# First stage of a hybrid decoder block: conditioning tiles loaded ahead of weight tiles, a quarter of three tiles' modulation products on TensorE, and a new hand-written order up to the second half's rows

## The chip, the cores and the metric

The program runs on one core of one Trainium2 chip. The metric is the device time of one execution in microseconds. Before the change three timed executions gave 1150.15, 1150.58 and 1151.71 us, median 1150.58 us.

The core has five instruction streams, each working through its own list in order: TensorE (PE, with its weight loads shown as PEld), VectorE (DVE), ScalarE (ACT), GpSimd (POOL) and SyncE (SP, which here only starts DMA transfers). A stream goes on to its next instruction only when what that instruction waits for has happened. So the order of each list matters as much as its length.

## The reference

The block has an input of 1024 rows (positions) by 1024 features, in float32, and a conditioning vector `c`. What the first stage has to compute is this part:

```python
c_act = jax.nn.silu(c)
mod = jnp.einsum('bd,de->be', c_act, w_ada[layer]) + b_ada[layer]
shift_m, scale_m, gate_m, shift_f, scale_f, gate_f = jnp.split(mod[:, None, :], N_MOD, axis=-1)
u = rms_norm(h, g_mix[layer]) * (1.0 + scale_m) + shift_m
proj = jnp.einsum('bsd,de->bse', u, w_in[layer])
u_pool, z = proj[..., OFF_POOL:OFF_Z], proj[..., OFF_Z:OFF_XBC]
u_xbc, u_dt = proj[..., OFF_XBC:OFF_DT], proj[..., OFF_DT:]
```

After it come a pooling mixer, a state-space mixer with a short causal convolution, an output projection and a squared-ReLU feed-forward part. They fill the rest of the execution, and the change doesn't touch them.

## The kernel before, in words

The rows are treated in two halves of 512 (row tiles 0 to 3 and 4 to 7, of 128 rows each). The 1024 features are eight tiles of 128, numbered `k`. Products in float32 are made as three products of split numbers: `hi` is the number rounded to TensorE's faster float32 form, `lo` is the rest, and `hi*hi + hi*lo + lo*hi` is summed.

**Opening, to about 17 us.** SP loads the first four row tiles (`tok`), then the first tile of input weights (`raw`, 128x768), then conditioning weights (`adaw`, one 128x8x256 tile for each `k`). For each row tile ACT squares and sums (`square_sum`), DVE divides (`rsqrt_cols`), POOL raises to the power -1/2 (`rst`), and DVE or ACT multiplies the row by it (`row_scale`). `cact` is silu(c), made on DVE from a transposed parameter tile. `busy(n)` are n products of ones whose result nobody reads.

**One feature tile `k`.** `ada_dve(k, ...)` on DVE forms the weighted sum over the eight slices of `adaw[k]`: two plain products, six multiply-and-adds into two accumulators (`adaa`), and for most `k` one addition of the two. `ada_pe(k)` on TensorE multiplies that by ones, which sums over partitions, and `ada_cols(k)` on DVE makes two columns of it, `sh_m` and `sc_m` (shift and scale). Then ACT, with these two columns, turns the transposed rows (`stage`) into `u` (its `hi` part) and `utmp`, and DVE subtracts for its `lo` part (`ada_lo`). The weight tile `raw` is cast to `hi` on ACT and subtracted to `lo` on DVE. `stage_x(k)` transposes the rows on TensorE and copies them on ACT.

**Chunks.** `chunk(k)`, for `k` 0 to 7, has 18 products of 128x512 on TensorE (`part`), into six PSUM banks `accs` that stay in use through the whole stage. Between them stand `stage_x(k + 2)`, the loads of tile `k + 2`, and the conditioning of tile `k + 1`: `ada_pe(k + 1)`, then `ada_hi`, `ada_lo`, `ada_dve(k + 2)`. So `ada_dve(k + 2)` stands on DVE behind the columns of `k + 1`, and the columns of `k + 2` need `ada_dve(k + 2)`.

**The second half's rows.** Tiles 4 to 7 are loaded in `chunk(5)`. `row_rs` and `row_scale` treat two of them after `chunk(6)` and two after `chunk(7)` (table `XS`). Then `z0_tok(t)` multiplies a row tile by the first z columns (24 products of 128x256), with weights `zu` in four units of `hi` and `lo`; `u_half1(k)` transposes and modulates the second half's rows; `conv_half` copies an `accs` bank to SBUF, which frees it; `feat` is a further 24 products of 128x512.

**What sets the order.** Inside `with pinned(...)` the listed engines keep the order of the program's lines. Outside, a scheduler may move instructions. Before, `chunk(0)` to `chunk(5)` are pinned on four engines, and chunks 6 and 7 are not pinned. The table `UH` says after which `z0_tok` which `u_half1` are placed. Buffers are limited: three for `adaw`, two for `raw`, three for `hi` and `lo`, eight PSUM banks.

Of the kernel before, what the change touches and what calls it, by code (L numbers as in the profile page):

```python
# [9 lines left out]
F32 = mybir.dt.float32  # L10
# [30 lines left out]
UH = ((), (), (0, 1), (2, 3, 4), (5, 6, 7))  # L41
NPF = 2
XS = {6: (4, 5), 7: (6, 7)}
# [22 lines left out]
def tile_hybrid_block(  # L66
# [282 lines left out]
    ada_a = {}  # L349

    def ada_dve(k, ks):
        if ks[0] == 0:
            ada_a[k] = [stp.tile([P, 256], F32, name="adaa", tag="adaa", bufs=4) for _ in range(2)]
        ada_reduce(ada_w[k], ada_a[k], 256, ks)
        if ks[-1] == KD - 1 and k > 1:
            a, b = ada_a[k]
            dve.tensor_tensor(out=a, in0=a, in1=b, op=ALU.add)
            ada_a[k] = [a]

    def ada_pe(k):  # L360
        ps = bank()
        pa, pb = ps[:, 0:HD], ps[:, HD:2 * HD]
        for f, p_ in enumerate((pa, pb)):
            fs = slice(f * P, (f + 1) * P)
            for i, a in enumerate(ada_a[k]):
                pe.matmul(p_, lhsT=a[:, fs], rhs=ones[:, 0:HD], start=i == 0, stop=i == len(ada_a[k]) - 1)
        ada_cols(k, pa, pb)
# [35 lines left out]
    kw = []  # L403
    with pinned((act, dve, pool, pe)):
# [9 lines left out]
        row_rs(0)  # L414
        row_scale(0, False)
        row_rs(1)
# [6 lines left out]
        row_rs(2)  # L423
# [6 lines left out]
        row_rs(3)  # L430
        row_scale(2, True, slice(HW, D))
        spec = specs.popleft()
        raw0 = stp.tile([P, 768], F32, name="raw", tag="raws", bufs=2)
        for c0, c1, src in spec[2]:
            sp.dma_start(out=raw0[:, c0:c1].unsqueeze(1), in_=src)
        ada_load(0)
        ada_load(1)
        acc = [stp.tile([P, 256], F32, name="adaa", tag="adaa", bufs=4)[:, :P] for _ in range(2)]
        hi0 = stp.tile([P, 768], F32R, name="hi", tag="hi", bufs=3)
        lo0 = stp.tile([P, 768], F32R, name="lo", tag="lo", bufs=3)  # L440

        def dve_f0(ks):
            for k in ks:
                a = acc[k % 2]
                src = ada_w[0][:, k, 0:P]
                if k < 2:
                    dve.tensor_scalar(out=a, in0=src, scalar1=cact[:, k:k + 1], scalar2=None, op0=ALU.mult)
                else:
                    dve.scalar_tensor_tensor(out=a, in0=src, scalar=cact[:, k:k + 1], in1=a,
                                             op0=ALU.mult, op1=ALU.add)  # L450
# [15 lines left out]

        lo_0(0, 384)
        pe_f1(range(2))
        busy(3)
        pe_f1(range(2, 4))  # L470
        busy(2)
        stage_x(0)
        pe_f1(range(4, 6))
        busy(1)
        pe_f1(range(6, KD))
        for i in range(2):
            pe.matmul(pa, lhsT=acc[i], rhs=ones[:, 0:HD], start=i == 0, stop=i == 1)
        ada_cols(0, pa, pb)
        tmp = ada_hi(0)
        lo_0(384, 768)  # L480
        ada_lo(0, tmp)
        stage_x(1)
        busy(WARM2)
        ada_dve(1, range(KD))
        kw.append([(hi0, lo0)])
        kw.append(get(1, 0))
        accs = [bank() for _ in range(6)]

    def part(k, f, i):
        whi, wlo = kw[k][0]  # L490
        u = uT[k][0]
        fs = slice(f * P, (f + 1) * P)
        w, v = ((whi, 0), (wlo, 0), (whi, 1))[i]
        pe.matmul(accs[f], lhsT=w[:, fs], rhs=u[:, v, :], start=k == 0 and i == 0, stop=k == KD - 1 and i == 2)  # L494
# [3 lines left out]
    def chunk(k):  # L498
        if k == 0:
# [5 lines left out]
        for f, i in todo[:6]:  # L505
            part(k, f, i)
        if k + 2 < KD:
            stage_x(k + 2)
            split = unit_load(*specs.popleft())
            ada_load(k + 2)  # L510
        for f, i in todo[6:cut]:
# [14 lines left out]
        if k == 5:  # L526
# [6 lines left out]
            zpre.extend(unit_load(*specs.popleft()) for _ in range(NPF))  # L533
# [4 lines left out]
        for t in XS.get(k, ()):  # L538
            row_rs(t, pool)
            row_scale(t, t == 7)  # L540
# [3 lines left out]
    chunk(6)  # L544
    chunk(7)
# [1106 lines left out]
```

## Time and profile before

| | us |
|---|---|
| median of three timed executions | 1150.58 |
| profiled execution, device time | 1151.4 |
| its span, first to last instruction | 1149.7 |
| PE busy | 1131.9 (98% of the span) |
| DVE busy | 828.6 (72%) |
| ACT busy | 564.2 (49%) |
| POOL busy | 147.6 (13%) |
| granted TensorE clock, mean | 0.998 |
| first product with weights (`part`) starts | 17.24 |
| columns of tile 7 (`sh_m`) start | 56.20 |
| first transposes for the second half start | 71.43 |

Times inside the execution are counted from the start of its span. A row of the timeline has the start, the duration, the engine, the line, the operation, `out<-in`, the shape, the count of merged instructions, and in brackets how long the engine was idle just before it and what ended that. Instructions on one engine overlap a little, so starts are compared with starts. A float32 product whose operands aren't split appears as two MATMUL instructions. An engine called SPq, ACTq or POOLq is that engine's queue of DMA starts.

### The profile page before, as it was taken

The numbers are of one execution on the slowest core, as the hardware profiler recorded it, in microseconds if no ns is written. First come the engines' busy times: TensorE is split into PE (matmuls) and PEld (weight loads), VectorE is DVE, ScalarE is ACT, GpSimd is POOL, SyncE is SP. The second block draws the span as 40 slices with busy tenths as digits, with TensorE's granted clock in tenths as the row PEclk, the third lists the DMA queues.
The fourth block names the chain that finished last, engine by engine and source line by source line (L and its number), as shares of the span: only waits on it lengthen the run. The fifth ranks groups of instructions, "written<-read, shape, count | busy, mean of one in ns | idle before, by whom it ended". The sixth has DMA issues, their size and how long they took to land.

```text
span 1149.7 us, 15130 instructions
## 1 busy us (share of the span) xinstructions
PE 1131.9 (98%) x5475; PEld 937.7 (82%) x5475; DVE 828.6 (72%) x1244; ACT 564.2 (49%) x988; POOL 147.6 (13%) x188
## 2 busy tenths in 40 slices
PE   8989999999999999999999999999999999999997
PEld 8788887877898878878788888888888888888886
DVE  6969889958778576666987666665458744586985
ACT  5577665534354424545774444444434344434373
POOL 3021235325300012022000000000100000000030
PEclk9999999999999999999999999999999999999999
DMA  9922432323166767763165434442599835775832
GB/s 281 306 62 74 131 101 80 94 87 106 67 190 195 230 189 230 242 198 114 36 238 195 172 139 164 144 158 88 211 387 342 306 93 161 251 250 188 269 125 92
DMA packets 124091, 200.72 MB, mean 175 GB/s; under 512 B 8656, under 2 KB 65776, under 8 KB 121968
## 3 DMA queue, kind: packets, MB, share of 16 engines
q1 hardware_dynamic: 122656, 196.24, 51.2%
q0 software_dynamic: 1120, 3.21, 0.8%
q8 instruction: 43, 0.70, 0.3%
q14 instruction: 32, 0.26, 0.1%
q10 hardware_dynamic: 240, 0.30, 0.1%
HBM read 159.81 MB, written 39.91 MB: 174 GB/s over the span
## 4 chain that ended last, share of the span: by engine, by line
PE 76%; DMA 9%; DVE 7%; ACT 3%; issue 2%; POOL 1%; SPq 0%; POOLq 0%; DVEq 0%; ACTq 0%
PE bank L240 67%; DMA raw<-in_w_ada_dram 4%; PE bank L760 2%; DMA raw<-in_w_out_dram 2%; PE bank L494 2%; DVE acc L868 2%; DMA adaw<-in_w_ada_dram 1%; DMA raw<-ypool_d 1%; DVE lo L192 1%; PE bank L764 1%; PE bank L134 1%; PE bank L757 1%; PE bank L835 1%; POOL rst L176 0%; ACT hi L191 0%
## 5 line engine op out<-in xcount | busy, mean ns | idle before, releaser
L240 PE MATMUL bank<-dlo,dhi 128*128 128x512 f32 (+1 forms) x464 | 177.2, 382 | 0.0
L240 PE MATMUL bank<-dhi 128*128 128x512 f32 (+1 forms) x464 | 177.2, 382 | 0.0
L240 PE MATMUL bank<-dhi,dlo 128*128 128x512 f32 (+1 forms) x464 | 177.1, 382 | 0.0
L240 PE MATMUL bank<-u,hi 128*128 128x512 f32 x464 | 149.6, 403 | 0.0
L1471 ACT CAST dhi<-fr 128x1024 fp32r<-128x1024 f32 x56 | 58.9, 1052 | 143.3 <-PE bank L240 110.0
L1472 DVE TENSOR_TENSOR dlo<-fr,dhi 128x1024 fp32r<-128x1024 f32 x56 | 68.5, 1223 | 80.4 <-ACT dhi L1471 80.2
L240 PE MATMUL bank<-hi,ym 128*128 128x512 f32 x384 | 124.4, 396 | 1.1 <-DVE tok L1089 1.1
L191 ACT CAST hi<-raw 128x512 fp32r<-128x512 f32 (+2 forms) x101 | 62.9, 633 | 87.2 <-DMA raw<-in_w_out_dram 39.7
L240 PEld LDWEIGHTS bank<-u,hi 128*128 128x128 f32 x464 | 85.9, 188 | 22.1 <-issue 4.8
L240 PEld LDWEIGHTS bank<-dhi 128*128 128x128 f32 x464 | 87.2, 188 | 17.1
L240 PEld LDWEIGHTS bank<-dlo,dhi 128*128 128x128 f32 x464 | 87.2, 188 | 16.9
L240 PEld LDWEIGHTS bank<-dhi,dlo 128*128 128x128 f32 x464 | 87.2, 188 | 16.7
L192 DVE TENSOR_TENSOR lo<-raw,hi 128x512 fp32r<-128x512 f32 (+2 forms) x101 | 74.8, 747 | 29.1 <-ACT hi L191 28.6
L240 PE MATMUL bank<-E,whl 128*128 128x512 f32 x384 | 92.6, 391 | 0.1
L240 PE MATMUL bank<-u,lo 128*128 128x512 f32 x232 | 90.7, 391 | 0.0
L240 PEld LDWEIGHTS bank<-hi,ym 128*128 128x128 f32 x384 | 72.1, 188 | 17.0 <-DVE tok L1089 1.5
L240 PEld LDWEIGHTS bank<-E,whl 128*128 128x128 f32 x384 | 71.7, 188 | 16.5 <-DVE whl L1245 0.9
L176 POOL TENSOR_TENSOR rst<-ssq,mhalf 128x1 f32<-128x1 f32 (+2 forms) x27 | 26.8, 995 | 395.8 <-DVE ssq L175 363.7
L240 PE MATMUL bank<-u,whl 128*128 128x512 f32 x312 | 75.6, 390 | 0.0
L240 PE MATMUL bank<-lo,ym 128*128 128x512 f32 x192 | 74.9, 390 | 0.3 <-DVE lo L192 0.3
L240 PEld LDWEIGHTS bank<-u,whl 128*128 128x128 f32 x312 | 58.5, 188 | 12.5 <-DVE whl L1245 0.4
L1245 DVE TENSOR_TENSOR whl<-wraw,whl 128x512 fp32r<-128x512 f32 x58 | 40.0, 689 | 36.9 <-ACT whl L1240 36.8
(272 smaller groups left out, 2200.7 us busy)
## 6 DMA issues: line engine op xcount, KB each, us to landing
f_d<-tok SPq DMA_DIRECT2D x16, 1792.0 KB, 7.0
wr<-in_w_down_dram SPq DMA_DIRECT2D x56, 512.0 KB, 5.1
fr<-f_d SPq DMA_DIRECT2D x53, 512.0 KB, 4.3
raw<-in_w_ada_dram SPq DMA_DIRECT2D x64, 256.0 KB, 3.1
wraw<-in_w_up_dram SPq DMA_DIRECT2D x15, 1024.0 KB, 5.3
raw<-in_w_in_dram SPq DMA_DIRECT2D x48, 256.0 KB, 3.3
raw<-in_w_out_dram SPq DMA_DIRECT2D x48, 256.0 KB, 3.3
tok<-in_x_dram SPq DMA_DIRECT2D x16, 512.0 KB, 5.9
```

The lines of the kernel that those rows point to most:

```text
L134: return pe.transpose(dst, src, ident)
L176: pool.tensor_tensor(out=rst[:, a:b], in0=m, in1=mhalf[:, :b - a], op=ALU.pow)
L191: act.copy(hi[:, :n], raw[:, :n])
L192: dve.tensor_tensor(out=lo[:, :n], in0=raw[:, :n], in1=hi[:, :n].bitcast(F32), op=ALU.subtract)
L240: pe.matmul(ps, lhsT=st_, rhs=mv, start=first and i == 0, stop=last and i == 2, skip_group_check=more)
L494: pe.matmul(accs[f], lhsT=w[:, fs], rhs=u[:, v, :], start=k == 0 and i == 0, stop=k == KD - 1 and i == 2)
L757: pe.matmul(po, lhsT=C[:, cs], rhs=states[g], start=True, stop=True)
L760: pe.matmul(py[:, hh * HD:(hh + 1) * HD], lhsT=Ms[hh // 4][:, (hh % 4) * P:(hh % 4 + 1) * P], rhs=xdt[:, hh * HD:(hh + 1) * HD], start=Tru ...
L868: dve.scalar_tensor_tensor(out=acc[0], in0=raw, scalar=cact[:, k:k + 1], in1=acc[0], op0=ALU.mult, op1=ALU.add)
L1245: dve.tensor_tensor(out=t_[:, 1], in0=src, in1=t_[:, 0].bitcast(F32), op=ALU.subtract)
L1471: act.copy(hi, src)
L1472: dve.tensor_tensor(out=lo, in0=src, in1=hi.bitcast(F32), op=ALU.subtract)
```

## The change

It does six things, all ahead of the second half's rows.

1. SP's list has the conditioning tile ahead of the weight tile throughout (`ada_load(0)`, `w_load()`, `ada_load(1)`, `w_load()`, ...).
2. For tiles 0, 1 and 2 the slices 6 and 7 of the weighted sum leave DVE. TensorE multiplies those two slices directly by a column of `cact` (`ada_pass`). Tile 2's two accumulators are summed on TensorE without DVE's addition (`ada_sum`), as those of tiles 0 and 1 already were.
3. `u`'s `hi` part is made by DVE for tiles 0 and 1.
4. The weight's cast stands ahead of the columns on ACT, and the weight's subtraction (`w_lo`) right behind the columns on DVE. Chunk 1 has the same order of products as chunk 0.
5. POOL starts four small parameter transfers a second time, between the powers of the first four rows.
6. Chunks 6 and 7 and the second half's rows are pinned on ACT, DVE and POOL. All four row tiles stand behind `chunk(7)`, all four units of z weights are loaded and split ahead of them, and `UH` starts one `z0_tok` earlier.

```diff
-UH = ((), (), (0, 1), (2, 3, 4), (5, 6, 7))
-NPF = 2
-XS = {6: (4, 5), 7: (6, 7)}
+UH = ((), (0,), (1, 2), (3, 4), (5, 6, 7))
...
+    direct = {0: (6, 7), 1: (6, 7), 2: (6, 7)}
...
+    def ada_pass(p_, k, i, f, start, stop):
+        pe.matmul(p_, lhsT=ada_w[k][:, i, f * P:(f + 1) * P], rhs=cact[:, i:i + 1].broadcast_to([P, HD]),
+                  start=start, stop=stop)
+
+    def ada_sum(p_, k, f, start, stop):
+        for i, a in enumerate(ada_a[k]):
+            pe.matmul(p_, lhsT=a[:, f * P:(f + 1) * P], rhs=ones[:, 0:HD], start=start and i == 0,
+                      stop=stop and i == len(ada_a[k]) - 1)
...
-        affine_act(u[:, 0, :], src, k)
-        (affine_dve if k == 0 else affine_act)(tmp, src, k)
-        return tmp
+        (affine_dve if k < 2 else affine_act)(u[:, 0, :], src, k)
+        return tmp, src
...
-        row_rs(0)
+        row_ssq(0)
+        row_pow(0)
+        pool.dma_start(out=pr1[80:84, :], in_=rows(pool_scale))
+        row_ssq(1)
         row_scale(0, False)
-        row_rs(1)
+        row_pow(1)
+        pool.dma_start(out=dtb, in_=dt_bias.broadcast_to([P, HEADS]))
...
+        row_ssq(2)
+        row_pow(2)
+        pool.dma_start(out=nea, in_=a_log.broadcast_to([P, HEADS]))
...
+        ada_dve(0, range(6))
         pe_f1(range(2))
...
+        ada_sum(pa, 0, 0, True, False)
         pe_f1(range(6, KD))
...
+        for k in (6, 7):
+            ada_pass(pa, 0, k, 0, False, k == 7)
         ada_cols(0, pa, pb)
...
         if k + 1 < KD:
+            w_hi(k + 1)
             ada_pe(k + 1)
-            tmp = ada_hi(k + 1)
-            if k + 2 < KD:
-                ada_dve(k + 2, range(4))
-            ada_lo(k + 1, tmp)
-            if k + 2 < KD:
-                ada_dve(k + 2, range(4, KD))
-                kw.append(split())
+            tmp, src = ada_hi(k + 1)
+            affine_act(tmp, src, k + 1)
+            w_lo(k + 1)
+            if k == 0:
+                ada_lo(k + 1, tmp)
+                ada_dve(k + 2, range(KD))
+            else:
+                if k + 2 < KD:
+                    ada_dve(k + 2, range(3))
+                ada_lo(k + 1, tmp)
+                if k + 2 < KD:
+                    ada_dve(k + 2, range(3, KD))
...
-            zpre.extend(unit_load(*specs.popleft()) for _ in range(NPF))
+            zpre.extend(unit_load(*specs.popleft()) for _ in range(4))
...
-        for t in XS.get(k, ()):
-            row_rs(t, pool)
-            row_scale(t, t == 7)
     with pinned((act, dve, pool, pe)):
         for k in range(6):
             chunk(k)
-    chunk(6)
-    chunk(7)
+    with pinned((act, dve, pool)):
+        chunk(6)
+        chunk(7)
+        for t in range(4, 8):
+            row_ssq(t)
+            row_pow(t, pool)
+            row_scale(t, t == 7)
```

The diff says little about where things come to stand, so here are three places of the built programs. Line numbers of the changed kernel differ from those of the kernel before.

First, DVE's list for one feature tile in the middle of the stage, from one pair of columns to the next, before (`adaa` are the accumulators of the following tile's weighted sum, `lo<-raw,hi` is the weight's subtraction, `u<-utmp,u` the rows' subtraction):

```order
L371 TENSOR_TENSOR sh_m<-bank,pc 128x1
L372 SCALAR_TENSOR_TENSOR sc_m<-bank,pc 128x1
L260 TENSOR_SCALAR adaa<-adaw,cact 128x256 x2
L262 SCALAR_TENSOR_TENSOR adaa<-adaw,cact,adaa 128x256 x2
L392 TENSOR_TENSOR u<-utmp,u 128x512
L262 SCALAR_TENSOR_TENSOR adaa<-adaw,cact,adaa 128x256 x4
L357 TENSOR_TENSOR adaa<-adaa 128x256
L192 TENSOR_TENSOR lo<-raw,hi 128x768
L371 TENSOR_TENSOR sh_m<-bank,pc 128x1
```

and the same stretch of the changed kernel:

```order
L384 TENSOR_TENSOR sh_m<-bank,pc 128x1
L385 SCALAR_TENSOR_TENSOR sc_m<-bank,pc 128x1
L475 TENSOR_TENSOR lo<-raw,hi 128x768
L258 TENSOR_SCALAR adaa<-adaw,cact 128x256 x2
L260 SCALAR_TENSOR_TENSOR adaa<-adaw,cact,adaa 128x256
L404 TENSOR_TENSOR u<-utmp,u 128x512
L260 SCALAR_TENSOR_TENSOR adaa<-adaw,cact,adaa 128x256 x5
L360 TENSOR_TENSOR adaa<-adaa 128x256
L384 TENSOR_TENSOR sh_m<-bank,pc 128x1
```

The weight's subtraction went from behind the last addition to ahead of the weighted sum, and nothing stands any more between that addition and the next columns.

Second, POOL's list in the opening. Before, from the last of the small transfers on (`rst` are the powers, one for each of the first four rows):

```order
L410 DMA adaa<-in_pool_scale_dram 4x128
L411 DMA dtb<-in_dt_bias_dram 128x16
L412 DMA nea<-in_a_log_dram 128x16
L413 DMA dsk<-in_d_skip_dram 128x16
L176 TENSOR_TENSOR rst<-ssq,mhalf 128x1 x4
```

and changed:

```order
L421 DMA adaa<-in_pool_scale_dram 4x128
L422 DMA dtb<-in_dt_bias_dram 128x16
L423 DMA nea<-in_a_log_dram 128x16
L424 DMA dsk<-in_d_skip_dram 128x16
L174 TENSOR_TENSOR rst<-ssq,mhalf 128x1
L427 DMA adaa<-in_pool_scale_dram 4x128
L174 TENSOR_TENSOR rst<-ssq,mhalf 128x1
L431 DMA dtb<-in_dt_bias_dram 128x16
L174 TENSOR_TENSOR rst<-ssq,mhalf 128x1
L440 DMA nea<-in_a_log_dram 128x16
L174 TENSOR_TENSOR rst<-ssq,mhalf 128x1
L449 DMA dsk<-in_d_skip_dram 128x16
```

The first list of transfers stayed whole. Each repeated one writes the same tile as its first copy, so it carries a wait for that copy to have landed, and the next row's power stands behind it.

Third, ACT's list from the modulation of feature tile 7 (`u`, `utmp`) to the first work on the second half's transposed rows. Before:

```order
L191 CAST hi<-raw 128x512 x2
L381 ACTIVATE u<-stage,sh_m,sc_m 128x512
L381 ACTIVATE utmp<-stage,sh_m,sc_m 128x512
L244 ACTIVATE utmp,ssq<-tok 128x1024 x4
L191 CAST hi<-raw 128x512
L323 ACTIVATE tok<-tok,rst 128x1024
L191 CAST hi<-raw 128x512 x3
L570 COPY craw<-bank 128x512 x2
```

and changed:

```order
L394 ACTIVATE utmp<-stage,sh_m,sc_m 128x512
L189 CAST hi<-raw 128x512 x4
L242 ACTIVATE utmp,ssq<-tok 128x1024 x4
L189 CAST hi<-raw 128x512
L323 ACTIVATE tok<-tok,rst 128x1024
L189 CAST hi<-raw 128x512
L645 ACTIVATE zt<-bank 128x240
L601 COPY craw<-bank 128x512 x2
```

Four casts of z weights now stand between `utmp` and the four squares (two of them stood ahead of `u`, and two behind the squares), and the two copies that free PSUM banks come behind one `zt` of the first z rows. On TensorE, the products of `z0_tok` that stood between the last parts of chunk 6 and of chunk 7 now stand behind chunk 7, and so does the rest of them.

More of the change, by code (lines that the diff above doesn't have):

```diff
@@ L349, in tile_hybrid_block @@
     ada_a = {}
+    direct = {0: (6, 7), 1: (6, 7), 2: (6, 7)}
     def ada_dve(k, ks):
+        own = [i for i in ks if i not in direct.get(k, ())]
         if ks[0] == 0:
-            ada_a[k] = [stp.tile([P, 256], F32, name="adaa", tag="adaa", bufs=4) for _ in range(2)]
-        ada_reduce(ada_w[k], ada_a[k], 256, ks)
-        if ks[-1] == KD - 1 and k > 1:
+            n = P if k == 0 else 256
+            ada_a[k] = [stp.tile([P, 256], F32, name="adaa", tag="adaa", bufs=4)[:, :n] for _ in range(2)]
+        ada_reduce(ada_w[k], ada_a[k], P if k == 0 else 256, own)
+        if ks[-1] == KD - 1 and k not in direct:
             a, b = ada_a[k]
@@ L362, in ada_pe @@
         pa, pb = ps[:, 0:HD], ps[:, HD:2 * HD]
+        own = direct.get(k, ())
         for f, p_ in enumerate((pa, pb)):
-            fs = slice(f * P, (f + 1) * P)
-            for i, a in enumerate(ada_a[k]):
-                pe.matmul(p_, lhsT=a[:, fs], rhs=ones[:, 0:HD], start=i == 0, stop=i == len(ada_a[k]) - 1)
+            for i in own:
+                ada_pass(p_, k, i, f, i == own[0], False)
+            ada_sum(p_, k, f, not own, True)
         ada_cols(k, pa, pb)
@@ L429, in tile_hybrid_block, with w_load, w_hi, w_lo @@
         row_scale(2, False, slice(0, HW))
-        row_rs(3)
+        row_ssq(3)
+        row_pow(3)
+        pool.dma_start(out=dsk, in_=d_skip.broadcast_to([P, HEADS]))
         row_scale(2, True, slice(HW, D))
[L432 to L435, printed above, removed]
         ada_load(0)
-        ada_load(1)
[L438 to L450, printed above, removed]
+        raws = {}
+        def w_load():
+            k = len(raws)
+            raw = stp.tile([P, 768], F32, name="raw", tag="raws", bufs=2)
+            for c0, c1, src in specs.popleft()[2]:
+                sp.dma_start(out=raw[:, c0:c1].unsqueeze(1), in_=src)
+            raws[k] = raw
+        w_load()
+        ada_load(1)
+        w_load()
+        whl = {}
+        def w_hi(k, parts=((0, 768),)):
+            if k not in whl:
+                whl[k] = [stp.tile([P, 768], F32R, name=n, tag=n, bufs=3) for n in ("hi", "lo")]
+            for c0, c1 in parts:
+                act.copy(whl[k][0][:, c0:c1], raws[k][:, c0:c1])
+        def w_lo(k, parts=((0, 768),)):
+            hi, lo = whl[k]
+            for c0, c1 in parts:
+                dve.tensor_tensor(out=lo[:, c0:c1], in0=raws[k][:, c0:c1], in1=hi[:, c0:c1].bitcast(F32),
+                                  op=ALU.subtract)
         pa, pb = bank()[:, 0:HD], bank()[:, 0:HD]
@@ L506, in chunk @@
             part(k, f, i)
+        if k == 0:
+            stage_x(1)
         if k + 2 < KD:
             stage_x(k + 2)
[L509 removed]
             ada_load(k + 2)
+            w_load()
         for f, i in todo[6:cut]:
```

41 lines of the change are left out of this document (17 added, 24 removed).

## The prediction

> **What bounds the kernel now.** I read the busy shares first:
>
> ```profile
> PE 1131.9 (98%) x5475; PEld 937.7 (82%) x5475; DVE 828.6 (72%) x1244; ACT 564.2 (49%) x988; POOL 147.6 (13%) x188
> ```
>
> TensorE is busy for 98% of the span; 17.8 us are left. So time can be won where TensorE waits, and lost wherever another engine makes it wait more. The shares don't say how close the others are in the changed stage. For that I read the timeline of one chunk, with DVE's steps and TensorE's modulation products among them:
>
> ```profile
> 33.61 0.16 DVE L371 TENSOR_TENSOR sh_m<-bank,pc 128x1 f32<-128x1 f32 x1
> ...
> 33.68 0.21 DVE L372 SCALAR_TENSOR_TENSOR sc_m<-bank,pc 128x1 f32<-128x1 f32 x1
> ...
> 33.81 0.61 DVE L260 TENSOR_SCALAR adaa<-adaw,cact 128x256 f32<-128x256 f32 x2
> ...
> 34.33 0.88 DVE L262 SCALAR_TENSOR_TENSOR adaa<-adaw,cact,adaa 128x256 f32<-128x256 f32 x2
> ...
> 35.54 0.69 DVE L392 TENSOR_TENSOR u<-utmp,u 128x512 fp32r<-128x512 f32 x1 [0.33 <-ACT utmp L381]
> ...
> 36.15 1.67 DVE L262 SCALAR_TENSOR_TENSOR adaa<-adaw,cact,adaa 128x256 f32<-128x256 f32 x4
> ...
> 37.85 0.42 DVE L357 TENSOR_TENSOR adaa<-adaa 128x256 f32<-128x256 f32 x1
> ...
> 38.20 0.95 DVE L192 TENSOR_TENSOR lo<-raw,hi 128x768 fp32r<-128x768 f32 x1
> ...
> 38.42 0.63 PE L366 MATMUL bank<-ones,adaa 128*128 128x64 f32 x4
> ...
> 39.09 0.16 DVE L371 TENSOR_TENSOR sh_m<-bank,pc 128x1 f32<-128x1 f32 x1
> ```
>
> The columns come 5.48 us apart (33.61 to 39.09), and this is a closed loop: columns, weighted sum with the rows' subtraction in it, addition (ends 38.27), products of ones (38.42 to 39.05), next columns. The weight's subtraction lies in the shade: DVE runs it while it would wait for those products. TensorE's side of one chunk, from the chain of waits:
>
> ```profile
> 39.05 2.96 PE bank L494 x12
> 42.01 0.44 PE bank L134 x4
> 42.45 1.40 PE bank L494 x6
> ...
> 43.91 0.63 PE bank L366 x4
> ```
>
> That is 5.43 us. TensorE and DVE's loop are 0.05 us apart here: what lengthens either lengthens the chunk. The waits that TensorE has in the first 130 us, from the view of waits (us in total, times, longest):
>
> ```profile
> PE bank L134 <- ACT cv L250: 1.1, 1, 1.1
> ...
> PE bank L240 <- DVE lo L192: 0.9, 1, 0.9
> ...
> PE bank L240 <- ACT hi L191: 0.9, 1, 0.9
> ...
> PE bank L494 <- ACT u L381: 0.8, 2, 0.4
> ...
> PE bank L366 <- DVE adaa L357: 0.5, 1, 0.5
> ```
>
> 4.2 us in all: the most that these edits could take from TensorE's visible waits behind the opening.
>
> **The change part by part.**
>
> *Opening.* The first copy of the transfer that POOL repeats first, its time from issue to landing, and what hangs on POOL's powers:
>
> ```profile
> 5.25 0.50 POOL L410 DMA_DIRECT2D adaa<-in_pool_scale_dram  x1
> ...
> 8.94 0.55 POOL L176 TENSOR_TENSOR rst<-ssq,mhalf 128x1 f32<-128x1 f32 x1 [0.93 <-DVE ssq L175]
> ...
> 9.53 0.75 DVE L325 TENSOR_SCALAR tok<-tok,rst 128x1024 f32<-128x1024 f32 x1 [0.33 <-POOL rst L176]
> ...
> 12.22 0.48 DVE L325 TENSOR_SCALAR tok<-tok,rst 128x512 f32<-128x512 f32 x1 [0.27 <-POOL rst L176]
> ...
> 12.63 1.84 DVE L449 SCALAR_TENSOR_TENSOR adaa<-adaw,cact,adaa 128x128 f32<-128x128 f32 x6
> ...
> 16.00 0.16 DVE L371 TENSOR_TENSOR sh_m<-bank,pc 128x1 f32<-128x1 f32 x1 [1.06 <-PE bank L477]
> ...
> 16.39 0.55 DVE L377 TENSOR_SCALAR utmp<-stage,sc_m,sh_m 128x512 f32<-128x512 f32 x1
> ...
> 17.24 1.67 PE L494 MATMUL bank<-u,hi 128*128 128x512 f32 x6 [0.39 <-ACT u L381]
> ```
>
> ```profile
> adaa<-in_pool_scale_dram POOLq DMA_DIRECT2D x1, 2.0 KB, 4.7
> ```
>
> The first copy lands at 5.25 + 4.7 = 9.95. The repeated one waits for that, then takes 0.50 to issue, so row 1's power starts at 10.45 and not at 8.94, and row 1's scaling on DVE at 11.1 and not at 9.53: +1.57. Behind the power stand the other powers; behind the scaling stand `cact`, the scaling of rows 2 and 3 and the weighted sum. Their old spacing (row 3's scaling 2.69 behind row 1's) leaves room for the other two issues if their copies, sent 0.5 and 1.1 us after the first, have landed too, which I take. Row 3 is scaled at 13.8. Now the whole weighted sum of tile 0 stands behind it, 0.41 later: two plain products (0.4) and four multiply-adds (two thirds of 1.84, 1.2) end at 15.85. Then TensorE has two products of ones and four direct ones to do. Their price is in the next fence: four products start 0.81 before the next thing, 0.2 each, so 1.2, and 0.3 for the wait and the tail. Columns at 17.35 instead of 16.00. `u` is now made by DVE (0.39 behind, 0.55 long) instead of ACT, so the first weight product is at 18.35: **+1.1**. The conditioning tile comes ahead of the weight tile, but it isn't what is late any more, so I cost that at nothing.
>
> *Tiles 1 and 2 on TensorE.*
>
> ```profile
> 21.06 1.00 PE L366 MATMUL bank<-ones,adaa 128*128 128x64 f32 x8
> ...
> 21.87 1.18 PE L494 MATMUL bank<-u,hi 128*128 128x512 f32 x4
> ...
> 28.12 0.16 DVE L371 TENSOR_TENSOR sh_m<-bank,pc 128x1 f32<-128x1 f32 x1
> ...
> 56.20 0.16 DVE L371 TENSOR_TENSOR sh_m<-bank,pc 128x1 f32<-128x1 f32 x1
> ```
>
> Tile 1 has four products of ones as before and four direct ones; tile 2 had two and gets eight. That is ten more, 2.0 us of TensorE. Along TensorE's order from 18.35: 14 parts (1.40/6 each, 3.3), two sets of transposes (0.9), eight products (1.6) and 0.2 give the columns of tile 1 at 24.3; 16 parts (3.7), one set (0.45), eight products (1.6) and 0.2 those of tile 2 at 30.3. DVE's own path from 24.3 (`u` 0.55, weight 0.95, rows 0.69, sum 2.3, then six products and the edges 1.6) gives 30.4. Before: 28.12, so **+2.2**, of which DVE's relief from two slices wins nothing back.
>
> *Tiles 3 to 7.* The weight's subtraction now stands between columns and weighted sum. That adds its 0.89 (38.20 to 39.09) to the loop and takes the 0.33 wait for `utmp` out, since `utmp` is done by then. The shade behind the addition stays empty: DVE waits there for the products as it must. 5.48 - 0.33 + 0.89 = 6.04, five times 30.2; TensorE's 5.43 fits inside and waits about 0.6 in each. Before, these five took 56.20 - 28.12 = 28.08 (five loops are 27.4, and one z weight's subtraction lay in the last). Columns of tile 7 at 60.5: **+4.3**.
>
> *From there to the second half.*
>
> ```profile
> 58.01 1.04 ACT L244 ACTIVATE utmp<-tok 128x1024 bf16<-128x1024 f32 x1
> ...
> 64.83 1.15 ACT L323 ACTIVATE tok<-tok,rst 128x1024 f32<-128x1024 f32 x1 [2.06 <-POOL craw L572]
> ...
> 65.89 1.64 ACT L191 CAST hi<-raw 128x512 fp32r<-128x512 f32 x3
> ...
> 71.43 1.03 PE L134 MATMUL bank<-ident,tok 128*128 128x128 f32 x8
> ...
> 83.29 1.47 PE L134 MATMUL bank<-ident,tok 128*128 128x128 f32 x12
> ```
>
> ```profile
> 72.47 2.87 PE bank L240 x24
> ```
>
> All z weights are split ahead of the first z product, so the two waits of 0.9 go. But the squares of the second half's rows now stand behind four casts (0.52 each, 2.1): 60.5 + 1.81 + 2.1 = 64.4. Row 7 is scaled 6.82 behind the first square, as before: 71.2. Then ACT has that scaling, a cast, one `zt` and the copy that frees the bank for the first transposes, 2.5 together: 73.7. TensorE alone would be there at 60.5 + 24 parts (5.6) + two z rows (2 x 2.9) = 71.9, so it waits 1.8. From the first transposes to the last twelve it was 71.43 to 83.29, 11.86, with the 1.1 wait in it. Now one z row more lies in this stretch: 11.86 - 1.1 + 2.9 = 13.7. The 1.1 may return since ACT and DVE come later: bounds 0 and 1.1, I take 0.5, as the transposes are spread out. The last twelve start at 73.7 + 14.2 = 87.9 instead of 83.3: **+4.6**.
>
> Behind it the lists are the same and TensorE is busy, so I carry 4.6 to the end. The profiled execution (span 1149.7, 1151.4 with what lies around it) would be 1156.0; the runs' median lies 0.8 below it, so 1150.58 + 4.6 = **1155.2 us**.
>
> **Rivals.**
>
> *The repeats hold nothing up.* If they don't wait, the opening is 1.57 earlier and everything behind it too: +3.0, 1153.6. For it: only 2 to 8 KB are moved. Against it: 4.7 us for just this transfer. The Trainium skill, "DMA: Bandwidth & Descriptors", section "Anatomy of one DMA — SWDGE (gpsimd) path", puts a transfer started by GpSimd at about 2.0 us plus its bytes; by that estimate the first copy would land at 7.3, and the result would be this rival's. The row is more than twice that, so the trace doesn't agree and I go by the row.
>
> *The second half's lag is hidden.* ACT doesn't hold the first transposes, and no bank is late: 71.9 + 13.7 = 85.6, +2.3, 1152.9. For it: POOL's backlog may be shorter when the squares start together. It decides if row 7 is scaled by 69.
>
> *TensorE alone decides, and it is faster.* The place is DVE's loop. If ACT's and DVE's work in the chunks stays in the shade, TensorE pays 2.0 more and loses its 4.2 us of waits, five times 0.05, and the 0.7 in the last chunk: -3.1, 1147.5. It decides from a loop under 5.43, so DVE would have to do the same steps 0.6 faster. For it: the chain is nearly all TensorE, and the 98%. Against it: the closed loop above. Its wait of 0.33 is all that DVE had free.
>
> *Worse still.* The other two repeats wait as well, or the 1.1 returns twice: up to 2 more, 1157.
>
> **How the numbers follow.** Two parts in a thousand, 2.3 us, are about what a measurement of this kernel tells from none. The forecast has 0.55 (its own range 1153.2 to 1157.2), the repeats 0.12, the hidden lag 0.15, TensorE alone 0.10, worse 0.08. Slower by over 0.2% (above 1152.9) gets 0.50 of the forecast, 0.09, 0.06 and 0.08: 0.73. Within 0.2%: 0.05, 0.03 and 0.09: 0.17. Faster: 0.10. The range is 1151.0 to 1157.6: it leaves out TensorE alone and little at either end.
>
> **What would show it.** Power of row 1 on POOL near 10.5, behind a transfer start that waited; first weight product near 18.4. Columns of tiles 2 to 7 about 6.0 apart, with TensorE's products of ones waiting some 0.6 for the addition; 5.5 there would make the prediction wrong, whatever the total. First transposes of the second half near 73.7, behind ACT's copy. If row 1's power is near 8.9, the repeats' rival holds; if TensorE shows no wait between tiles 3 and 7, TensorE's does.

## The result, and the profile after

| | before | after |
|---|---|---|
| median of the timed executions, us | 1149.70 (8) | 1154.85 (8) |
| lowest and highest | 1148.71 to 1151.71 | 1153.74 to 1161.72 |
| ratio, with its 95% interval | | 1.0060 (1.0046 to 1.0074) |
| profiled execution: device time, span | 1151.4, 1149.7 | 1157.49, 1155.8 |
| granted TensorE clock in it, mean | 0.998 | 0.996 |

The change makes the kernel slower: by 5.15 us between the medians, and by 5.3 to 8.5 us by the interval of the ratio. The ratio lies above that of the medians because three of the eight executions took over 1157 us; the means are 6.6 apart. The forecast was 1155.2 us. The changed kernel's executions differ with their mean granted clock: of twelve, seven at 0.997 or 0.998 took 1153.7 to 1155.2 us and five at 0.992 to 0.996 took 1157.5 to 1161.7. The total is right, but four of the five terms that make it up are off by 0.6 to 1.7 us, and part of the profiled time comes from a mechanism that the prediction doesn't have. So the closeness of the total is partly luck.

The busy shares of the changed kernel, from the page of its profile:

```profile
PE 1136.4 (98%) x5497; PEld 942.5 (82%) x5497; DVE 827.0 (72%) x1238; ACT 563.8 (49%) x988; POOL 150.3 (13%) x192
```

They tell next to nothing: still 98%. PE has 22 more instructions and 4.5 us more, and DVE six instructions fewer. The timeline tells more. First the opening: POOL's list, and DVE's and TensorE's rows that hang on it.

```profile
10.83 0.56 POOL L427 DMA_DIRECT2D adaa<-in_pool_scale_dram  x1 [2.83 <-DMA adaa<-in_pool_scale_dram]
11.40 0.57 POOL L174 TENSOR_TENSOR rst<-ssq,mhalf 128x1 f32<-128x1 f32 x1
11.92 0.95 POOL L431 DMA_DIRECT2D dtb<-in_dt_bias_dram  x1
...
13.44 0.67 POOL L440 DMA_DIRECT2D nea<-in_a_log_dram  x1
...
14.66 0.68 POOL L449 DMA_DIRECT2D dsk<-in_d_skip_dram  x1
```

```profile
12.01 0.75 DVE L325 TENSOR_SCALAR tok<-tok,rst 128x1024 f32<-128x1024 f32 x1 [2.45 <-POOL rst L174]
...
13.50 0.49 DVE L325 TENSOR_SCALAR tok<-tok,rst 128x512 f32<-128x512 f32 x1 [0.46 <-POOL rst L174]
...
14.73 0.49 DVE L325 TENSOR_SCALAR tok<-tok,rst 128x512 f32<-128x512 f32 x1 [0.68 <-POOL rst L174]
...
18.08 0.16 DVE L384 TENSOR_TENSOR sh_m<-bank,pc 128x1 f32<-128x1 f32 x1 [1.42 <-PE bank L364]
```

```profile
12.95 0.66 PE L364 MATMUL bank<-cact,adaw 128*128 128x64 f32 x4 [0.95 <-DVE cact L442]
...
19.16 1.63 PE L515 MATMUL bank<-u,hi 128*128 128x512 f32 x6 [0.62 <-DVE u L390]
```

POOL stands for 2.83 us at the first repeated transfer. The views of the first copy (line L421, started at 5.24) and of the repeat (L427) tell when that copy landed:

```profile
DMA to landing us min/median/max: 5.0/5.0/5.0
...
L427 POOLq EVENT_SEMAPHORE  x1: 17/17/17, 10.3 to 10.3; - x1
```

The copy has landed, and POOL's wait is met, at 10.2 to 10.3; the repeat starts at 10.83, 0.5 us later. Row 1's power starts at 11.40 instead of 8.94, and the first product with weights at 19.16 instead of 17.24.

Next, one turn of DVE's loop in the middle of the stage:

```profile
37.55 0.16 DVE L384 TENSOR_TENSOR sh_m<-bank,pc 128x1 f32<-128x1 f32 x1 [0.81 <-PE bank L369]
...
37.75 0.95 DVE L475 TENSOR_TENSOR lo<-raw,hi 128x768 fp32r<-128x768 f32 x1
...
39.54 0.68 DVE L404 TENSOR_TENSOR u<-utmp,u 128x512 fp32r<-128x512 f32 x1
...
42.24 0.42 DVE L360 TENSOR_TENSOR adaa<-adaa 128x256 f32<-128x256 f32 x1
43.48 0.16 DVE L384 TENSOR_TENSOR sh_m<-bank,pc 128x1 f32<-128x1 f32 x1 [0.81 <-PE bank L369]
```

The columns come 5.93 us apart instead of 5.48. The weight's subtraction (`lo`) stands between columns and weighted sum, and DVE idles for 0.81 where it used to stand. TensorE's waits up to 130 us (the view of waits: total, times, longest):

```profile
PE bank L369 <- DVE adaa L360: 2.0, 4, 0.5
PE bank L132 <- ACT craw L601: 1.8, 1, 1.8
...
PE bank L515 <- ACT u L394: 1.0, 1, 1.0
PE bank L364 <- DVE cact L442: 1.0, 1, 1.0
```

And TensorE at the second half's first transposes:

```profile
74.52 0.66 PE L132 MATMUL bank<-ident,tok 128*128 128x128 f32 x4 [1.80 <-ACT craw L601]
...
79.37 1.04 PE L132 MATMUL bank<-ident,tok 128*128 128x128 f32 x8
...
90.39 1.47 PE L132 MATMUL bank<-ident,tok 128*128 128x128 f32 x12
```

Between the first two of these rows lie 24 products of 128x256. The kernel before needed 2.9 us for such a row of z. Here it takes 4.4. The view by stretches of time shows why (stretch, its length, PE busy and its products, granted clock, share of the DMA engines, GB/s):

```profile
74.00:75.00 1.00, 0.48 (x5) 1.00 0.00 0
75.00:76.00 1.00, 1.00 (x7) 0.52 0.28 52
76.00:77.00 1.00, 1.00 (x7) 0.50 0.71 210
77.00:78.00 1.00, 1.00 (x7) 0.50 0.03 8
78.00:79.00 1.00, 1.00 (x8) 0.78 0.00 0
```

For about 3.4 us behind the wait of 1.80 TensorE has half its clock. The kernel before has 1.00 in all these stretches.

Where the time of the two profiles parts, from starts of the columns (`sh_m`) and of the transposes:

| stretch | before | after | difference | predicted |
|---|---|---|---|---|
| to the columns of tile 0 | 16.00 | 18.08 | +2.08 | +1.35 |
| to the columns of tile 2 | 12.12 | 13.54 | +1.42 | +0.83 |
| to the columns of tile 7 | 28.08 | 29.64 | +1.56 | +2.12 |
| to the first transposes of the second half | 15.23 | 13.26 | -1.97 | -2.03 |
| to the last twelve transposes | 11.86 | 15.87 | +4.01 | +2.34 |
| sum | 83.29 | 90.39 | +7.10 | +4.61 |

### The profile page after: what moved, and what is told of

It reads as the page before. It is cut to its first block, busy times and chain, and to the rows that moved or that the text cites. A ratio compares the mean times of both kernels' runs of the same rounds, so it can differ in the third digit from the quotient of the medians.

```text
span 1155.8 us, 15183 instructions
## 1 busy us (share of the span) xinstructions
PE 1136.4 (98%) x5497; PEld 942.5 (82%) x5497; DVE 827.0 (72%) x1238; ACT 563.8 (49%) x988; POOL 150.3 (13%) x192
## 4 chain that ended last, share of the span: by engine, by line
PE 77%; DMA 8%; DVE 7%; ACT 3%; issue 3%; POOL 2%; SPq 0%; POOLq 0%; ACTq 0%; DVEq 0%
PE bank L238 68%; DMA raw<-in_w_ada_dram 4%; PE bank L791 2%; DMA raw<-ypool_d 1%; DVE acc L899 1%; PE bank L795 1%; PE bank L515 1%; PE bank L788 1%; PE bank L132 1%; DMA adaw<-in_w_ada_dram 1%; DVE lo L190 1%; DMA raw<-in_w_out_dram 1%; POOL rst L174 1%; PE bank L866 1%; POOL tok L1046 0%
## 5 line engine op out<-in xcount | busy, mean ns | idle before, releaser
L189 ACT CAST hi<-raw 128x512 fp32r<-128x512 f32 (+1 forms) x94 | 57.2, 619 | 81.9 <-DMA raw<-in_w_out_dram 46.1
L190 DVE TENSOR_TENSOR lo<-raw,hi 128x512 fp32r<-128x512 f32 (+1 forms) x94 | 69.3, 745 | 29.3 <-ACT hi L189 28.7
```

The source lines that it names most:

```text
L189: act.copy(hi[:, :n], raw[:, :n])
L190: dve.tensor_tensor(out=lo[:, :n], in0=raw[:, :n], in1=hi[:, :n].bitcast(F32), op=ALU.subtract)
```

## The experiments

In all of them but two the changed kernel is the base. "The last twelve" are the last twelve transposes, which stood at 83.29 before and at 90.39 after. Each kernel was compared with the kernel before on the same chip.

### The opening: the repeats taken out, and put into the kernel before

The changed kernel without the four repeats:

```diff
         row_pow(0)
-        pool.dma_start(out=pr1[80:84, :], in_=rows(pool_scale))
...
         row_pow(1)
-        pool.dma_start(out=dtb, in_=dt_bias.broadcast_to([P, HEADS]))
...
-        pool.dma_start(out=nea, in_=a_log.broadcast_to([P, HEADS]))
...
-        pool.dma_start(out=dsk, in_=d_skip.broadcast_to([P, HEADS]))
```

> The changed kernel without the four repeated POOL transfers; nothing else differs. Theory (the repeats wait for their first copies and hold up the row powers, and TensorE carries the delay to the end): row 1's power goes from 11.40 back to about 8.94, the first weight product from 19.16 to about 16.8, the period of the columns of tiles 3 to 7 stays 5.93, and the time falls by about 2.3 us, from 1154.85 to 1152.5. Rival (the delay is given back later, because the conditioning tiles are loaded meanwhile): the first weight product moves, but the twelve transposes of the second half stay within 0.5 us of 90.39 and the time within 0.5 us of 1154.85.

Measured: 1152.65 us, ratio 1.0029 (1.0015 to 1.0043), 2.2 below the changed kernel's median. Columns of tile 0:

```profile
15.56 0.16 DVE L384 TENSOR_TENSOR sh_m<-bank,pc 128x1 f32<-128x1 f32 x1 [1.42 <-PE bank L364]
```

That is 2.52 earlier, and the last twelve stand at 87.87, also 2.52 earlier. So the delay of the repeats goes to the last twelve undiminished. One pair of profiles tells its size only roughly: the other profiles with this opening and the repeats have the columns at 18.0 to 18.5 (and one at 20.3 with half the clock), the other two without the repeats at 15.5 and 16.2. So whether the new opening without repeats is ahead of the old one's 16.00 stays open.

The reverse, the kernel before with the same four lines behind its four `row_rs`:

> The kernel before, with only the four repeated transfers on POOL added, each behind the power of its row. My theory: row 1's power moves from 8.9 to about 11 us, the columns of tile 0 from 16.0 to 18 or a little above, and the delay stays to the end: 1.9 to 2.3 us more, about 1151.9 to 1152.3. Rival, an opening with slack (the weights' transfers are what the first products wait for): under 0.7 us more, 1150.3 or less.

Measured: 1150.18 us, ratio 1.0014 (1.0005 to 1.0024), 1.17 above the kernel before. My number of 1.9 to 2.3 is missed, and so is the rival's difference of under 0.7 (its time, 1150.3 or less, is met, since the kernel before took 1149.01 here). Its rows:

```profile
11.18 0.57 POOL L176 TENSOR_TENSOR rst<-ssq,mhalf 128x1 f32<-128x1 f32 x1
```

```profile
17.10 0.16 DVE L371 TENSOR_TENSOR sh_m<-bank,pc 128x1 f32<-128x1 f32 x1
```

Row 1's power is 2.24 late (8.94 before), yet the columns only 1.10 (and the last twelve 0.90). In the kernel before the columns waited 1.06 for TensorE; that wait is gone in this row, so it was slack, and it swallowed half of the delay. The new order has no such slack: its whole weighted sum stands behind row 3's scaling, and TensorE's sums and direct products behind that, so the columns wait the same 1.42 for TensorE with and without the repeats. By these profiles the same four transfers cost 1.1 us in the old order and 2.5 in the new one.

### The loop: four kernels for the place of the weight's subtraction

The kernel before, with only that subtraction moved (`lows` holds it back until the next columns):

```diff
             tmp = ada_hi(k + 1)
+            if lows:
+                lows.pop()()
             if k + 2 < KD:
...
-                kw.append(split())
+                kw.append(split(lows))
```

> The kernel before, with only the weight's subtraction of tiles 2 to 7 moved on DVE from behind the addition to right behind the next columns (ACT's split stays where it was). My theory of the loop: in each of the steps from tile 2 to tile 7 the columns come 5.48 - 0.33 (the rows' subtraction no longer waits) + 0.8 to 0.89 apart, 5.95 to 6.04 instead of 5.48, so 2.3 to 2.8 us in five steps, and most of it stays to the end: 1151.3 to 1152.3 where the kernel before takes 1149 to 1149.7. Rival: the loop isn't closed through DVE, TensorE's 5.43 hides the move: under 0.5 us more.

Measured: 1151.45 us, ratio 1.0012 (1.0003 to 1.0022), 1.84 above the kernel before; columns of tile 7 1.97 later and the last twelve 1.96 later, at 85.25. A turn, and the waits:

```profile
33.72 0.16 DVE L373 TENSOR_TENSOR sh_m<-bank,pc 128x1 f32<-128x1 f32 x1 [0.81 <-PE bank L368]
...
33.92 0.95 DVE L193 TENSOR_TENSOR lo<-raw,hi 128x768 fp32r<-128x768 f32 x1
...
38.40 0.42 DVE L359 TENSOR_TENSOR adaa<-adaa 128x256 f32<-128x256 f32 x1
39.64 0.16 DVE L373 TENSOR_TENSOR sh_m<-bank,pc 128x1 f32<-128x1 f32 x1 [0.81 <-PE bank L368]
```

```profile
PE bank L368 <- DVE adaa L359: 2.2, 5, 0.5
```

This one edit makes the whole of the changed kernel's period: 5.92, and TensorE waits five times. From the addition to the next columns it is 1.24 here (38.40 to 39.64), 1.24 before (37.85 to 39.09) and 1.24 after (42.24 to 43.48): what stands in that gap is free, and what is taken out of it is paid. From tile 2 to tile 7 it is 2.31 more, at the lower end of what I gave. The step from tile 1 to tile 2 came out 0.40 shorter, which leaves 1.97.

Then the changed kernel with the subtraction put back ahead of the columns:

```diff
             w_hi(k + 1)
+            if k > 0:
+                w_lo(k + 1)
             ada_pe(k + 1)
...
-            w_lo(k + 1)
             if k == 0:
+                w_lo(k + 1)
```

> The changed kernel with the weight's subtraction of tiles 2 to 7 put back ahead of the columns on DVE (behind the addition); nothing else differs. Theory (the subtraction stands in DVE's closed loop): the columns of tiles 3 to 7 come 5.4 to 5.5 us apart instead of 5.93, TensorE's waits of 0.5 for the addition go, and the time falls by about 2.5 us, to 1152.3. Rival (TensorE sets the pace): the distance stays above 5.8 and the time within 0.5 us of 1154.85.

Measured: 1156.46 us, ratio 1.0060 (1.0045 to 1.0075); no gain. The columns are 5.88 apart:

```profile
38.52 0.48 DVE L260 SCALAR_TENSOR_TENSOR adaa<-adaw,cact,adaa 128x256 f32<-128x256 f32 x1
39.73 0.69 DVE L404 TENSOR_TENSOR u<-utmp,u 128x512 fp32r<-128x512 f32 x1 [0.73 <-ACT utmp L394]
```

The subtraction is back in the gap, but now the rows' subtraction waits 0.73 for ACT, against 0.33 in the kernel before. The change had also cut the multiply-adds ahead of it from two to one; with `lo` ahead of them that was free, without it they were the cover. So both are undone together (in the next two kernels `range(3)` becomes `range(4)`):

> The changed kernel with two edits undone together in the chunks of tiles 2 to 7: the weight's subtraction stands ahead of the columns again (behind the addition), and four multiply-adds instead of three stand between columns and the rows' subtraction. My theory of the loop: columns 5.48 apart from tile 3 to tile 7 (5.93 changed, 5.88 with the first edit alone), no wait of the rows' subtraction beyond 0.35, five times 0.45 = 2.2 us less, time about 1152.7. Rival: the second copy of u on ACT is late for another reason (ACT splits the weight ahead of it), the subtraction still waits 0.4 or more, columns stay above 5.8 apart, time about 1154.5.

Measured: 1156.16 us, ratio 1.0062 (1.0046 to 1.0077), above both times that I gave. The wait is back at 0.33, but the columns are 5.61 apart, between the theory and its rival:

```profile
41.69 0.43 DVE L360 TENSOR_TENSOR adaa<-adaa 128x256 f32<-128x256 f32 x1
42.18 0.96 DVE L475 TENSOR_TENSOR lo<-raw,hi 128x768 fp32r<-128x768 f32 x1
```

From the addition to `lo` it is 0.49; in the kernel before 0.35 (37.85 to 38.20). On ACT the split that `lo` needs runs from 41.31 to 42.15, behind the copy of the transposed rows. One more kernel puts that split ahead of the copy:

```diff
+        if 0 < k < KD - 1:
+            w_hi(k + 1)
         if k + 2 < KD:
             stage_x(k + 2)
...
-            w_hi(k + 1)
+            if k == 0:
+                w_hi(k + 1)
```

> The changed kernel with the weight's subtraction ahead of the columns and four multiply-adds ahead of the rows' subtraction (columns were 5.61 apart so), and ACT's split of the weight ahead of its copy of the transposed rows instead of behind it. If the 0.13 that was left came from the subtraction waiting for ACT's split, the columns come 5.48 to 5.50 apart; rival: they stay 5.6 apart. Columns of tile 7 about 19.4 us behind those of tile 3 plus 6.15 for the last step, against 23.7 for the four steps of the changed kernel: 1.2 us less to the last twelve transposes, which a time of 1153.5 to 1154 would show.

Measured: 1153.97 us, ratio 1.0034 (1.0021 to 1.0047).

```profile
41.53 0.43 DVE L360 TENSOR_TENSOR adaa<-adaa 128x256 f32<-128x256 f32 x1
41.87 0.95 DVE L475 TENSOR_TENSOR lo<-raw,hi 128x768 fp32r<-128x768 f32 x1
42.77 0.16 DVE L384 TENSOR_TENSOR sh_m<-bank,pc 128x1 f32<-128x1 f32 x1
```

The columns are 5.48 to 5.49 apart, the old period, and the changed loop is accounted for: what it loses is 0.33 of idle time and 0.08 of overlap (0.41), what it gains 0.86 of subtraction, and a late split makes 0.13 in the kernel ahead of this one. The changed kernel itself, on the same chip:

> The changed kernel itself once more, beside the two others on one chip: 1154.0 to 1155.5, and columns of tile 0 between 18.0 and 18.5.

It took 1156.49 us, above what I gave, ratio 1.0052 (1.0036 to 1.0068); columns of tile 0 at 18.03, the last twelve at 90.57. Repairing the loop so wins 2.88 at the last twelve: the columns of tile 7 come 1.73 earlier behind those of tile 0 (41.67 and 43.40), those of tile 0 were 0.20 later, and 1.35 more come because this profile has no half clock behind the wait at the first transposes. That second part is not the loop's.

### Direct products for tile 0 alone

```diff
-    direct = {0: (6, 7), 1: (6, 7), 2: (6, 7)}
+    direct = {0: (6, 7)}
```

> The changed kernel with direct products for tile 0 alone; tiles 1 and 2 have all eight slices on DVE again. Theory (DVE's loop and TensorE's list are about even in these two tiles): DVE gets 0.86 more in each and an addition in tile 2, TensorE 2.0 less; columns of tile 1 about 0.65 earlier, tile 2's distance 6.5 instead of 6.32, together -0.4 us, 1154.4. Rival (the prediction's plain sum, in which the ten products are on TensorE's path and DVE's relief is worth nothing): -2.0 us, 1152.9. Other rival (the relief of DVE is worth more than the products): +1 us or more.

This also gives tiles 1 and 2 an addition on DVE, so TensorE has two products for each of them instead of eight. Measured: 1155.31 us, ratio 1.0055 (1.0036 to 1.0075), no lower than the changed kernel; a term of 0.3 us can't be told from the total. Counted from the columns of tile 0, those of tile 1 come 0.57 earlier than in the changed kernel, those of tile 2 0.30, those of tile 7 0.32. For tile 1 the six products more cost 0.57; for tile 2 they win 0.27, since without them TensorE waits for DVE:

```profile
30.76 0.63 PE L369 MATMUL bank<-ones,adaa 128*128 128x64 f32 x4 [1.37 <-DVE adaa L360]
```

So the direct products of tiles 1 and 2 cost 0.3 us together. A plain sum of TensorE's extra products, 2.0, is wrong, since most of it lies where DVE would be late.

### The second half: the old order, and a mixed one

The old tables and the unpinned chunks 6 and 7 put back, everything else as changed:

```diff
-UH = ((), (0,), (1, 2), (3, 4), (5, 6, 7))
+UH = ((), (), (0, 1), (2, 3, 4), (5, 6, 7))
+NPF = 2
+XS = {6: (4, 5), 7: (6, 7)}
```

> The changed kernel with the second half's rows as before the change: chunks 6 and 7 not pinned, two z units loaded ahead, two rows treated behind chunk 6 and two behind chunk 7, and the old table for the second half's transposes. Theory (ACT's squares behind four casts are late for the first transposes, and that outweighs the z waits that went): from the columns of tile 7 to the last twelve transposes 27.1 us as before instead of 29.1, z waits of about 0.9 and 0.9 back, and the time falls by about 2.0 us, to 1152.9. Rival (the new order there is neutral or a gain, and all the loss lies ahead of it): the stretch stays 28.6 or longer and the time within 0.5 us of 1154.85 or above.

Measured: 1155.88 us, ratio 1.0062 (1.0039 to 1.0085); not lower. The two waits of the z products are back (0.9 and 0.8), the one of 1.8 is gone, and there is a new one at the columns of tile 7, which come 7.28 behind those of tile 6 instead of 5.93:

```profile
61.23 0.69 DVE L192 TENSOR_TENSOR lo<-raw,hi 128x512 fp32r<-128x512 f32 x1
61.83 0.42 DVE L362 TENSOR_TENSOR adaa<-adaa 128x256 f32<-128x256 f32 x1
```

```profile
62.40 0.63 PE L371 MATMUL bank<-ones,adaa 128*128 128x64 f32 x4 [0.87 <-DVE adaa L362]
```

A z weight's subtraction now stands ahead of DVE's last addition, where nothing covers it. From the columns of tile 6 to the last twelve it is 34.38 here, 35.06 in the changed kernel and 33.24 before. Behind the columns of tile 7 the stretch is 27.10, as the theory has it; the 1.35 lost ahead of them it doesn't have.

Then the changed kernel with rows 4 and 5 behind two of the four z splits, and rows 6 and 7 behind one more each (`half_row` is square, power and scaling of a row tile):

```diff
-            ready.extend(f() for f in zpre)
+            ready.extend(f() for f in zpre[:2])
+            half_row(4)
+            half_row(5)
...
+        for t in (6, 7):
+            ready.append(zpre[t - 4]())
+            half_row(t)
```

> The changed kernel with rows 4 and 5 of the second half squared and scaled behind two of the four z weights' splits, and rows 6 and 7 behind one more each. In the changed kernel TensorE waits 1.8 us for ACT ahead of the second half's first transposes, and then runs at a granted clock of 0.5 for about 3.4 us. If the wait is what brings the half clock: no wait over 1 us between the columns of tile 7 and the last twelve transposes, granted clock 1.00 throughout, the 24 products behind the first transposes 2.9 us long instead of 4.4, first transposes 12.5 us behind the columns of tile 7 instead of 13.26, the last twelve 27.4 us behind them instead of 29.1; time 1.8 us less, about 1153.0 to 1154.5. Rival, the half clock comes from the place or the load and not from the wait: it shows again, and the last twelve come 28.5 us or more behind the columns.

In the second half all of it came as the theory has it: no wait above 1.0, first transposes 12.47 behind the columns of tile 7, the last twelve 26.96 behind them instead of 29.13, and full clock:

```profile
75.00:76.00 1.00, 0.90 (x8) 1.00 0.62 184
76.00:77.00 1.00, 1.00 (x11) 1.00 0.56 118
77.00:78.00 1.00, 1.00 (x10) 1.00 0.91 237
```

But the time was 1157.62 us, ratio 1.0073 (1.0059 to 1.0087), against 1153.0 to 1154.5 expected. The profile has the half clock elsewhere, in the opening:

```profile
13.01 0.66 PE L364 MATMUL bank<-cact,adaw 128*128 128x64 f32 x4 [1.72 <-DVE cact L442]
...
21.39 2.90 PE L515 MATMUL bank<-u,hi 128*128 128x512 f32 x6 [0.16 <-DVE u L390]
```

```profile
12.00:16.00 4.00, 2.56 (x19) 0.94 1.03 283
16.00:20.00 4.00, 4.00 (x21) 0.50 1.07 297
20.00:24.00 4.00, 3.84 (x12) 0.50 0.66 165
24.00:28.00 4.00, 4.00 (x21) 0.78 0.96 262
```

TensorE waited 1.72 us there for `cact`, which hangs on row 1's scaling and so on the repeats, and from 15.5 on it ran at half clock for some 10.2 us (0.48, 4, 4 and 1.76 us at 0.50 give the four means). That this wait is the cause isn't shown: in the kernel with subtraction and four multiply-adds put back the same wait is 1.70, and the clock stays at 1.00 behind it. Columns of tile 1 at 29.58 instead of 25.30: 4.3 us in a stretch whose lines the edit doesn't touch. Whether that edit wins anything in time can't be told from these runs.

### Toward a better kernel

No repeats, direct products for tile 0 alone, the loop with subtraction and four multiply-adds put back:

> The changed kernel without the repeats, with direct products for tile 0 alone, and with the weight's subtraction and four multiply-adds put back as above. If the terms add up: 1154.9 - 2.2 (repeats) - 2.2 (loop) - 0.3 (direct products) = 1150.2, the same as before the change within 0.2%; columns 15.6 at tile 0 and then 5.48 apart from tile 2 on. Rival: one gain hides another, since TensorE takes 5.43 in a chunk and the second half's rows are held by ACT: 1151.5.

Measured: 1151.97 us, ratio 1.0020 (1.0011 to 1.0030). That is 2.9 below the changed kernel and not the 4.7 that I added up; the rival's 1151.5 is nearer. Columns at 16.17 for tile 0 and 5.61 apart from tile 2 on: the late split was not known yet. The last twelve stand at 86.10.

And the mixed second half on top:

> As the run before it, and the second half's rows 4 and 5 are squared and scaled behind two of the four z weights' splits, and rows 6 and 7 behind one more each, instead of all four rows behind all four splits. If ACT's four casts ahead of the squares hold the first transposes (wait of 1.8 us), that wait falls under 0.5 and the time is 1.3 lower than that of the run before it, about 1148.9. Rival, the squares aren't what holds them (the chain from POOL's powers over row 7's scaling to ACT's copies has its own length): within 0.4 of the run before it.

Measured: 1151.94 us, ratio 1.0024 (1.0013 to 1.0035), the same as the run before it; the rival is right. The wait of 1.8 is gone, and from the columns of tile 7 to the last twelve it is 27.36 instead of 27.74. Of the 0.78 won at the first transposes 0.38 went into a longer wait behind them (0.80 against 0.42), and there was no half clock to save in the run before it:

```profile
77.90 0.66 PE L132 MATMUL bank<-ident,tok 128*128 128x128 f32 x4 [0.80 <-DVE cv L250]
```

No kernel here beats the kernel before.

## Why the prediction was right, point by point

- **The repeats wait** (right, under-sized). Row 1's power was to start at 10.45 and started at 11.40; row 3 was to be scaled at 13.8 and was at 14.73; the first weight product came 1.9 later instead of 1.1. The term that was too small is the time up to the repeat: I let it start when the first copy lands, and took 4.7 us for that. The copy took 5.0, and 0.5 us more passed before the repeat started (5.6 us behind the copy's start, 5.24 to 10.83), which the prediction doesn't have. In the nine profiles with repeats the landing takes 4.8 to 5.4 and the gap behind it is 0.5 to 0.6. The rest of the working held: from row 1's scaling to row 3's 2.72 against 2.69. The rival that the repeats hold nothing up is out by the run without them.
- **Tiles 1 and 2** (+1.42 against +0.83). The first turn took 7.22 against 6.95 worked out, the second 6.32 against 6.0. Little pieces were each too short: eight products took 1.7 and not 1.6, the first weight product stands 1.08 behind the columns and not 1.0, and in the second turn it is 4.4 from the columns to the direct products and not 4.15.
- **The loop** (right, over-sized). 5.93 against 6.04. Two terms were mis-sized: the wait that goes is 0.41 between starts, of which the bracket shows 0.33, and the subtraction takes 0.86 from start to start and not 0.89. TensorE's products of ones wait 0.50, in four of the five turns; 0.6 was expected. With the edit alone in the kernel before the period is 5.92, so this step is shown and not only argued.
- **ACT holds the first transposes** (right). 1.80 measured, 1.8 predicted, first transposes 13.26 behind the columns of tile 7, 13.2 predicted; the 0.5 kept for stalls behind them measured 0.46. The rival of the hidden lag is out.
- **What the prediction doesn't have**: the half clock behind that wait. It takes the 24 products from 2.9 to 4.4 us, and the stretch to the last twelve from about 14.5 (three profiles with the same wait and no half clock: 14.50, 14.53 and 14.88, the last with 0.4 more of waits behind) to 15.87. It makes 1.4 of the 2.5 us by which the profile is above my sum at that place.
- **TensorE alone, and faster** is out: four waits of 0.5 between tiles 3 and 7, where the kernel before has none.
- **The end.** 4.6 predicted, 5.15 between the medians, 7.1 at the last twelve, 6.1 in the span. That 4.6 is near the medians is in part luck: the sum lacks 1.3 for the opening and tiles 1 and 2, has 0.6 too much for the loop and nothing for the half clock, and most timed executions ran at a higher clock than the profiled one. From the last twelve on the lists are the same, but that rest differs by up to 3.5 us between profiles (1062.9 and 1065.4 in the two profiles of the changed kernel, 1066.4 in the kernel before), so a term under 1 us can't be checked by the total.

## What to carry to other kernels

An instruction in a closed loop is free where its engine waits anyway, and costs its full length a few places up the same list; find that gap (here 1.24 us between addition and columns, in the kernel before, in the changed one and with the one edit between them) before moving anything, and look what the moved instruction covered at its old place. A transfer started again into the same tile makes its in-order queue wait for the first copy, and what stands behind it in the list pays, by as much as that order has no slack: 1.1 us in one order, 2.5 in the other. And a TensorE wait of well over a microsecond may cost more than itself: price the clock behind it too.

## What the runs showed of the hardware

**Half clock behind a wait of TensorE.** Eight profiles have a wait of 1.77 to 1.80 at the second half's first transposes. In five (the changed kernel twice, without repeats, and two of the loop) the granted clock falls to 0.50 for about 3.4 us, starting 1.9 to 2.3 us behind the start of the wait; in three it stays at 1.00. The kernel before with repeats has such a stretch too, much later: a wait of 2.22 up to 418.59, then half clock from 418.81 to 422.22. In the opening a wait of 1.72 was followed by half clock for some 10.2 us, but only 4.2 us behind its start; waits of 1.70 and 1.65 there, and one of 1.68 at 421 us (all in kernels with the loop put back), were followed by none. So a wait of this length makes it possible and doesn't settle it; what does is open.

The traces do show a fixed window behind it. In every profile the clock falls once more at the very end, when TensorE has nothing left to do. In all seven profiles with an earlier fall the two falls are a whole number of windows of 3.4133 us apart: 75.04 and 1150.23 in the changed kernel (315 windows), 418.81 and 1145.85 in the kernel before with repeats (213), 15.52 and 1152.16 in the last experiment on the second half (333), where the half clock lasts three windows. But the window alone doesn't explain why the same wait does it in one kernel and not in another: counted back from the end, all eight waits of 1.77 to 1.80 lie wholly inside one window. In the five that brought half clock the wait ended 0.1 to 0.5 us ahead of the window's end, in the three others 0.02, 0.74 and 0.76; no run tells whether that is the reason. The Trainium skill, "TensorE: Matmul & The Clock Gate", section "What's actually happening", has a free-running window of 3413 ns by which the clock goes to half and back; the traces agree. The Trainium skill, on the same page, section "HAM oscillation — how this bites in real kernels", warns of idle gaps above some 3.4 us; here 1.8 us was enough in five profiles of eight.

The mean clock of single executions points at the opening. One stretch of 3.4 us at half clock takes 0.0015 off the mean, so from the usual 0.998 a mean of 0.995 or less would need more than one. Of 40 executions of kernels with the new opening and the repeats 11 had that, of the 23 without repeats none, though two of those three kernels have the wait of 1.8. The kernel before had it once in 59 executions, and once in nine with the repeats.

**A transfer's start on POOL takes longer under a DVE operation.** The repeated start of `dtb` took 0.95 us (first copy 0.59), from 11.92 to 12.87, while DVE scaled a row from 12.01 to 12.76; those of `nea` and `dsk` took 0.67 and 0.68 under DVE's rows of 13.50 and 14.73, and each ends 0.11 to 0.12 behind DVE's end. The first repeat, with DVE idle, took 0.56. The Trainium skill, "SBUF — State Buffer", section "A bandwidth-pool intuition that's wrong (but worth ruling out)", gives a transfer that GpSimd starts under a DVE copy as blocked until DVE's end and about 115 ns; the trace agrees, under a DVE scaling.
